# Attention's order from a list of tasks, with tile 2's threshold updates on GpSimd

## The chip, the cores and the metric

The kernel runs on one core of a Trainium2 chip. Its time is the device time of one execution in microseconds, 1262.98 us as the median of three (1262.89 to 1263.99). Five engines work beside each other, each through its own queue in a fixed order, and wait for one another by semaphores: TensorE (PE in the profile, PEld for its weight loads), VectorE (DVE), ScalarE (ACT), GpSimd (POOL) and SyncE (SP, which only issues transfers).

## The reference

One decoder layer on 1024 tokens of width 1024 in float32. A projection of the scaled and shifted input gives queries, keys and values of 8 heads of 64, an indexer's queries and keys, and channels for a causal pool. Attention is sparse: for each query token the indexer scores all earlier tokens, and only the 256 best stay.

```
score = einsum('bqh,bqhs->bqs', w, relu(logits))
score = where(causal, score, -inf)
_, idx = top_k(score, 256)
...
s = einsum('bqhd,bqkhd->bhqk', qb, kg) * HEAD_DIM ** -0.5
p = softmax(where(valid, s, -inf))
o = einsum('bhqk,bqkhd->bqhd', p, vg)
```

Attention and pool are concatenated and multiplied by w_o, then come a layer norm, a SwiGLU feed-forward part and a second layer norm.

## The kernel before

Tokens are cut into eight tiles of 128 (tile i holds tokens 128i to 128i + 127). A tile's 256 best are found as a threshold: 31 bits are settled one after another, each by a count of the scores that reach a candidate, taken over the tile's row of 128(i + 1) scores. `bisect` (line 565) is a Python generator that writes this search step by step; at each `yield` it names the engine of its next piece and a price. `search_v` (596) counts on VectorE and then moves the candidate with two instructions on a column of 128 numbers, `pr` and `cand`; `search_a` (610) does the same on ScalarE. `TILES_A` and `TILES_V` (37) share the tiles out: 3, then 5 and 4 on ScalarE, 7 and 6 on VectorE, and tile 2, alone, on VectorE (`LATE`, 45). Tiles 0 and 1 need no search. When it is done, the scores of the tile hold 0 where a token stays and a large negative number elsewhere, and are added as a mask.

Searches are filled into other work: `Queue` (131) stands in front of every engine, prices each instruction, and before it issues one asks `fill` (697) whether a piece of an open search fits into the engine's idle time. Tile 2's search waits until the one of tiles 7 and 6 is done. What is `pinned` for an engine keeps the order in which it was written; the rest is ordered by the framework's own scheduler, which lets an instruction that is ready pass one that isn't, by its own prices. During attention nothing is pinned.

Attention is 32 units (`units`, 1013): a group g of two tiles (2g + 1 and 2g, from g = 3 down), four head pairs pr in each, and for each pair the two tiles. A unit goes through five steps:

- `u_scores` (1017): TensorE, queries times keys for both heads into a PSUM tile of two banks per head (two such tiles exist, so one unit of tiles 7 to 4 fills both; tiles 3 to 0 take one for both heads).
- `u_exp` (1029): VectorE adds the mask and takes the maximum in one instruction per head, ScalarE the exponential and its sum. `need` (693) first drives the tile's search to its end.
- `u_norm` (1047): VectorE's reciprocal, and GpSimd's multiplication of the probabilities.
- `u_trans` (1055): TensorE transposes blocks of 128, up to four to a PSUM bank, and each bank is copied to `ptb`, every fourth copy by VectorE and the rest by ScalarE.
- `pair_pv` and `pair_cat` (1072, 1082): after both tiles of a pair, TensorE multiplies by the values; ScalarE copies the high part, VectorE makes the low part.

Before these loops only queries of tiles 7 and 6 are ready. `q_make` (934) makes those of the others when group g is under way: the raw rows come back from memory, TensorE transposes them, ScalarE writes four pieces, VectorE two low parts. The places are in `qab` (925); tile 0 shares tile 3's. A matrix product in this kernel takes high and low parts of its operands, so each operand exists twice.

The loop from line 1125 writes the order: scores two units ahead, the finished pair's product, normalisation two units ahead, then this unit's transposes (`STEP_ORDER`, 44). In the last seven units the first blocks of w_o are loaded (`wo_load`, 1092, with GpSimd's multiplication by the gate) and split (`wo_split`, 1097). Behind attention the product with w_o starts (`first`, 1520).

## Time and profile before

| | us |
|---|---|
| median of three runs | 1262.98 |
| profiled execution | 1263.04 |
| its span, first to last instruction | 1261.3 |
| TensorE busy | 1193.2 |
| VectorE busy | 1005.1 |
| ScalarE busy | 662.6 |
| GpSimd busy | 709.0 |

A row of the profile gives the engine, the operation, what it writes and reads (out<-in, with a letter for the area of the on-chip memory), shapes, a count, busy time and mean duration, and the idle time of the engine before it with what ended it. Nearly all rows carry line 174, since every instruction goes through `Queue`; so work is told by its tiles. In attention, `s` are the scores, `sm_H` the probabilities, `pT` and `pT_H` the transposed ones in PSUM and copied, `o` the product with the values, `ws_W` its parts, `qT` and `qab` the queries, `stat_X` maxima and sums. `junk_X`, `keysA_X` and `colsE_X` are tile 2's search, `junkB_X` and `colsA_X` tile 3's. Busy time of TensorE includes the end of each matmul, which the next one overlaps, so a busy TensorE isn't one at its peak.

### The profile page before, as it was taken

Reading aid. Unit: us, or ns where it says so; the run is one execution under the profiler, and the core shown is the slowest. Engines: PE = TensorE matmul, PEld = TensorE weight load, DVE = VectorE, ACT = ScalarE, POOL = GpSimd, SP = SyncE. Lnnn points to the kernel's source line nnn. Section 1 sums busy time; section 2 is a strip of 40 time slices with the busy share of each in tenths; the row PEclk is TensorE's granted clock in tenths of the full one; section 3 lists DMA queues with packets and bytes.
Section 4 is the critical chain, followed back from the end, with each engine's and each line's share of the span. In section 5 each row is a group of like instructions: output and inputs, shape, how many; then the busy total and the mean of one; then the engine's idle time right before and its main releaser. Section 6 shows DMA issues by size and latency. Waiting matters only on the chain.

```text
span 1261.3 us, 16420 instructions
## 1 busy us (share of the span) xinstructions
PE 1193.2 (95%) x5622; PEld 923.9 (73%) x5622; DVE 1005.1 (80%) x1842; ACT 662.6 (53%) x1351; POOL 709.0 (56%) x505
## 2 busy tenths in 40 slices
PE   8999999999888999996889999999999999999996
PEld 6756556687656667885778787878778787878775
DVE  6799997989998765776877868787877778687698
ACT  4667878888785894455443334343333333333521
POOL 0193474675132464285684848384756657486848
PEclk9999999999997999997999999999999999999998
DMA  9610167411000044100202020101111020202112
GB/s 355 240 51 17 58 245 272 155 48 59 17 10 9 26 167 167 60 9 23 102 27 84 32 70 34 67 34 68 39 62 68 34 84 34 84 34 101 63 55 117
DMA packets 32459, 103.40 MB, mean 82 GB/s; under 512 B 3572, under 2 KB 3572, under 8 KB 28792
## 3 DMA queue, kind: packets, MB, share of 16 engines
q1 hardware_dynamic: 32376, 102.36, 22.5%
q8 instruction: 44, 0.72, 0.2%
q14 instruction: 39, 0.32, 0.1%
HBM read 92.90 MB, written 9.45 MB: 81 GB/s over the span
## 4 chain that ended last, share of the span: by engine, by line
PE 63%; DVE 19%; POOL 7%; ACT 6%; issue 5%; DMA 1%; SPq 0%; DVEq 0%; POOLq 0%; ACTq 0%
PE gu L174 23%; PE dn L174 15%; PE pj L174 7%; PE wo L174 4%; DVE junk_X L174 3%; PE pair L174 3%; PE pT L174 2%; DVE act_W L174 2%; PE o L174 2%; PE s L174 2%; DVE utmp_X L174 2%; PE lg L174 2%; POOL wraw_R L174 2%; PE iq L174 1%; DVE stat_C L174 1%
## 5 line engine op out<-in xcount | busy, mean ns | idle before, releaser
L174 PE MATMUL gu<-hr_H,wblk_T 128*128 128x512 f32 (+1 forms) x924 | 217.1, 387 | 5.1 <-ACT gtmp_V L174 4.0
L174 PE MATMUL gu<-hr_H,wblk_V 128*128 128x512 f32 (+1 forms) x924 | 216.3, 386 | 2.4 <-ACT gtmp_V L174 1.8
L174 PEld LDWEIGHTS gu<-hr_H,wblk_T 128*128 128x128 f32 x924 | 171.5, 190 | 41.6 <-ACT gtmp_V L174 4.8
L174 PEld LDWEIGHTS gu<-hr_H,wblk_V 128*128 128x128 f32 x924 | 170.7, 189 | 38.8 <-ACT gtmp_V L174 2.2
L174 DVE TENSOR_TENSOR res_X<-res_X,dn 128x512 f32<-128x512 f32 (+1 forms) x253 | 158.5, 677 | 15.5 <-PE dn L174 15.3
L174 POOL TENSOR_TENSOR wraw_R<-wraw_R 128x512 f32<-128x512 f32 x64 | 94.2, 1480 | 45.8 <-DVE wblk_T L174 23.1
L174 POOL TENSOR_TENSOR wraw_W<-wraw_W 128x512 f32<-128x512 f32 x60 | 86.1, 1442 | 56.8 <-DVE wblk_V L174 28.7
L174 PE MATMUL pj<-ws_W,hT_H 128*128 128x512 f32 x456 | 115.6, 400 | 1.0 <-DVE ws_W L174 1.0
L174 POOL TENSOR_SCALAR sm_H<-sm_H,stat_X 128x1024 f32<-128x1024 f32 (+7 forms) x64 | 48.8, 776 | 113.5 <-PE s L174 42.1
L174 PEld LDWEIGHTS pj<-ws_W,hT_H 128*128 128x128 f32 x456 | 83.0, 188 | 24.9 <-issue 6.6
L174 PE MATMUL dn<-wblk_T,act_W 128*128 128x512 f32 x324 | 79.8, 395 | 2.6 <-DVE act_W L174 1.4
L174 PE MATMUL dn<-wblk_V,act_W 128*128 128x512 f32 x324 | 79.1, 393 | 1.1 <-POOL wblk_V L174 1.1
L174 DVE TENSOR_SCALAR_CACHE_REDUCE junk_X<-keysD_T,colsD_X 128x1024 int16<-128x1024 int16 (+1 forms) x64 | 79.5, 1269 | 0.2
L174 ACT ACTIVATE wblk_V<-wraw_R 128x512 fp32r<-128x512 f32 x56 | 35.2, 629 | 79.5 <-POOL wraw_R L174 66.9
L174 PEld LDWEIGHTS dn<-wblk_T,act_W 128*128 128x128 f32 x324 | 60.6, 189 | 18.3 <-POOL wblk_T L174 3.9
L174 ACT ACTIVATE wblk_V<-wraw_W 128x512 fp32r<-128x512 f32 x53 | 33.1, 628 | 75.1 <-POOL wraw_W L174 61.7
L174 PEld LDWEIGHTS dn<-wblk_V,act_W 128*128 128x128 f32 x324 | 60.1, 188 | 16.6 <-POOL wblk_V L174 3.9
L174 ACT ACTIVATE wblk_T<-wraw_W 128x512 fp32r<-128x512 f32 x56 | 34.9, 627 | 67.2 <-POOL wraw_W L174 56.2
L174 ACT ACTIVATE wblk_T<-wraw_R 128x512 fp32r<-128x512 f32 x52 | 32.5, 627 | 62.0 <-POOL wraw_R L174 52.0
L174 DVE SCALAR_TENSOR_TENSOR score_X<-relu_K,const_C,score_X 128x384 f32<-128x384 f32 (+5 forms) x42 | 54.1, 1289 | 5.0 <-ACT relu_K L174 1.4
L174 ACT ACTIVATE utmp_X<-gu 128x512 f32<-128x512 f32 x33 | 19.8, 599 | 72.7 <-PE gu L174 72.7
L174 ACT ACTIVATE junkA_T<-keys_T,colsA_X 128x768 bf16<-128x768 uint16 (+3 forms) x62 | 54.4, 877 | 3.8 <-DVE colsA_X L174 2.9
(299 smaller groups left out, 2747.0 us busy)
## 6 DMA issues: line engine op xcount, KB each, us to landing
mset_K<-in_wmr_dram SPq DMA_DIRECT2D x16, 1024.0 KB, 5.4
wm_K<-in_wma_dram SPq DMA_DIRECT2D x16, 512.0 KB, 9.9
wraw_R<-in_wg_dram SPq DMA_DIRECT2D x6, 1024.0 KB, 4.8
wraw_R<-in_wd_dram SPq DMA_DIRECT2D x12, 512.0 KB, 3.5
wraw_W<-in_wup_dram SPq DMA_DIRECT2D x12, 512.0 KB, 3.5
wraw_R<-in_wup_dram SPq DMA_DIRECT2D x10, 512.0 KB, 3.6
wraw_W<-in_wg_dram SPq DMA_DIRECT2D x5, 1024.0 KB, 4.9
wraw_W<-in_wd_dram SPq DMA_DIRECT2D x10, 512.0 KB, 3.5
```

The lines of the kernel that those rows point to most:

```text
L174: ins_ = f(*a, **k)
```

## The change

Attention is no longer written by a loop. Every step of every unit, every set of queries and every pair's product becomes a `Task` with an engine, a price, a rank, the tasks that it follows and the PSUM slots that it takes (`Ring`: four of one bank, two of two banks). Searches still open are `Chain`s, whose next step has a rank that spreads what is left of them up to one unit before the tile is wanted. A loop then takes, again and again, what can start first by the prices, and of those that can start at the same time the lowest rank; it writes that one and moves its engine's clock. All of it is pinned on TensorE, VectorE, ScalarE and GpSimd. A copy of transposed blocks goes to either ScalarE or VectorE, VectorE with 0.15 us against it. Queries have a rank 40 below the unit that uses them; tile 0's get a place of their own. The first w_o blocks are written behind attention, not pinned. And the two column instructions that end each step of tile 2's search go to GpSimd.

```diff
 AHEAD = 2
+EAGER = 0
+Q_LEAD = 40
+CHAIN_LEAD = 1
+V_BIAS = 0.15
...
-                    yield "V", 0.3 + 1.08 * w_(i) + (0.35 * nt if m == nt - 1 else 0.0)
+                    yield "V", 0.3 + 1.08 * w_(i) + (0.35 * nt if m == nt - 1 and tiles != LATE else 0.0)
...
                 off = -float(1 << (b - 1)) if b > 0 else -1.0
+                by = V
+                if tiles == LATE:
+                    by = G
+                    yield "G", 0.45
                 for m in range(nt):
-                    V.tensor_scalar(one(pr, m), one(cntc, m), 0.0, float(1 << b), ALU.is_ge, ALU.mult)
+                    by.tensor_scalar(one(pr, m), one(cntc, m), 0.0, float(1 << b), ALU.is_ge, ALU.mult)
                 for m in range(nt):
-                    V.tensor_scalar(one(cand, m), one(pr, m), one(cand, m), off, ALU.add, ALU.add)
+                    by.tensor_scalar(one(cand, m), one(pr, m), one(cand, m), off, ALU.add, ALU.add)
...
-        streams.insert(0, [T.t, next(b), b, a[0], a[0] == LATE])
+        streams.insert(0, [T.t, next(b), b, a[0], a[0] == LATE, a[2], 0])
...
+    class Task:
+
+        def __init__(self, q, cost, rank, emit, deps=(), slots="", late=0.0):
+            self.q, self.cost, self.rank, self.emit, self.deps, self.slots, self.late = q, cost, rank, emit, deps, slots, late
+            self.end, self.kind, self.masks = None, emit.__name__[0:2], ()
+
+    class Ring:
+
+        def __init__(self, n):
+            self.free = [[0.0] for _ in range(n)]
+
+        def ready(self, n):
+            return max((f[0] if f[0] is not None else FAR) for f in self.free[0:n])
+
+        def take(self, n):
+            got = [[None] for _ in range(n)]
+            self.free = self.free[n:] + got
+            return got
...
-    for u in units[0:AHEAD]:
-        u_scores(u)
-        u_exp(u)
+    qab[0] = buf("T", 0, 1536, "qab", F32R)
...
+    def q_rows(t, rank):
...
+        l_ = task("S", 0.1, rank, load, q_turns[-3:-2], late=4.0)
+        t_ = task("T", 0.55, rank, turn, (l_,), "A", late=0.2)
+        c0 = task("A", 1.2, rank, lambda: copies(0), (t_,))
+        lw = task("V", 1.4, rank, lambda: copies(2), (c0,))
+        c1 = task("A", 1.2, rank, lambda: copies(1), (c0,))
+        t_.readers = (c1, lw)
+        t_.masks = {1: (2, 3), 0: (4, 5)}.get(t, ())
...
+        s_t = task("T", 0.1 + 0.0014 * n, 10 * k - EAGER, s_, q_done[i], "B" if n <= 512 else "BB", late=0.2)
+        before = [t for w in where for t in sm_users.get(w, ())]
+        xs = [task("V", 0.08 + 0.00105 * n, 10 * k, lambda e=e: x_(e), [s_t] + before, late=0.12) for e in (0, 1)]
+        for x in xs:
+            x.masks = (i,)
+        s_t.readers = xs
+        es = [task("A", 0.16 + 0.00097 * n, 10 * k + 1, lambda e=e: e_(e), (xs[e],), late=0.15) for e in (0, 1)]
+        r_ = task("V", 0.15, 10 * k + 1, lambda: V.reciprocal(cols["c"][:, 2:4], cols["c"][:, 2:4]), es, late=0.15)
+        ns = [task("G", 0.1 + 0.001 * n, 10 * k + 2, lambda e=e: n_(e), (r_,), late=0.15) for e in (0, 1)]
...
+                p = task("T", 0.107 * m, 10 * k + 3, p_, (ns[e],), "A", late=0.25)
+                c = task("AV", (0.09 + 0.11 * m, 0.09 + 0.13 * m), 10 * k + 3, c_, [p] + list(o_tasks[-2:-1]), late=0.1)
+                p.readers = (c,)
...
+    Q_USE = {5: 8, 4: 9, 3: 16, 2: 17, 1: 24, 0: 25}
+    for t in (5, 4, 3, 2, 1, 0):
+        q_rows(t, 10 * Q_USE[t] - Q_LEAD)
...
+        o_t = task("T", 0.1 + 0.43 * (g + 1), 10 * k + 14, o_, cs, "A", late=0.3)
+        h_t = task("A", 0.3, 10 * k + 15, hi_, (o_t,), late=0.1)
+        l_t = task("V", 0.38, 10 * k + 16, lo_, (h_t,), late=0.1)
...
+    goal = {2: 17, 3: 16, 4: 9, 5: 8, 6: 1, 7: 0}
+    class Chain:
+
+        def __init__(self, st):
+            self.st, self.at, self.n = st, 0.0, -1
+            nt = len(st[3])
+            total = 6 * nt + 1 + (31 * (nt + 1) + 2 if st[5] else 31 * nt)
+            self.left = max(total - st[6], 1)
+            self.goal = max(goal[i] for i in st[3]) - CHAIN_LEAD
+            self.step()
+
+        def step(self):
+            self.n += self.q != "G" if self.n >= 0 else 1
+            self.rank = 10 * self.goal * (self.n + 1) / self.left
+            self.q = self.st[1][0]
+            self.cost = 1.08 * self.st[1][1]
...
-    for st in streams:
-        st[4] = True
-    u_norm(units[0])
-    nxt, nrm = AHEAD, 1
-    for n_, u in enumerate(units):
-        g, pr, i = u
-        for step in STEP_ORDER:
-            if step == "S":
-                while nxt < nu and nxt <= n_ + (AHEAD if units[nxt][0] > 1 else AHEAD_SMALL):
-                    u_scores(units[nxt])
-                    u_exp(units[nxt])
-                    nxt += 1
-            elif step == "P" and i % 2 == 1 and n_ > 0:
-                pair_cat(*units[n_ - 1][0:2], pair_pv(*units[n_ - 1][0:2]))
-            elif step == "N":
-                while nrm < nu and nrm <= n_ + (NORM if units[nrm][0] > 1 else NORM_SMALL):
-                    u_norm(units[nrm])
-                    nrm += 1
-            elif step == "T":
-                u_trans(u)
-        if g > 0 and (pr, i % 2) in Q_AT:
-            t = 2 * (g - 1) + 1 - Q_AT.index((pr, i % 2))
-            q_make(t, q_load(t))
-        if g == 0 and n_ == nu - 7:
-            wo_load(0)
-        if g == 0 and n_ == nu - 5:
-            wo_split(0)
-            wo_load(1)
-            wo_load(2)
-    while streams:
-        advance(streams[0])
+    pinned.update("TVAG")
...
+    def earliest(t, q):
+        at = clock[q]
+        for d in t.deps:
+            if d.end is None:
+                return FAR
+            at = max(at, d.end)
+        for i in t.masks:
+            if i not in masked:
+                return FAR
+            at = max(at, masked[i])
+        if t.slots:
+            at = max(at, rings[t.slots[0]].ready(len(t.slots)))
+        return at
...
+    while todo or chains:
+        best = None
+        for t in todo:
+            if best is not None and t.rank > best[3] + 400:
+                break
+            for n_q, q in enumerate(t.q):
+                at = earliest(t, q)
+                if at >= FAR:
+                    continue
+                key = (at + (V_BIAS if n_q else 0.0), t.rank)
+                if best is None or key < best[0]:
+                    best = key, t, q, t.rank, at, n_q
+        for c in chains:
+            at = max(clock[c.q], c.at)
+            key = (at, c.rank)
+            if best is None or key < best[0]:
+                best = key, c, c.q, c.rank, at, 0
...
+        cost = (t.cost[n_q] if type(t.cost) is tuple else t.cost) + 0.02
+        if q == "T":
+            cost += 0.15 * (kind[0] != t.kind)
+            kind[0] = t.kind
...
+    pinned.clear()
+    wo_load(0)
+    wo_split(0)
+    wo_load(1)
+    wo_load(2)
     times.fill = None
     wo_split(1)
-    pair_cat(0, 3, pair_pv(0, 3))
     wo_split(2)
     for k in range(3, KT):
         wo_load(k)
```

More of the change, by code (lines that the diff above doesn't have):

```diff
@@ L683, in advance @@
             pinned.add(q.name)
+        st[6] += 1
         try:
@@ new lines, in decoder_layer_kernel, with task @@
+    FAR = 1.0e9
+    todo, rings = [], {"A": Ring(4), "B": Ring(2)}
+    def task(*a, **k):
+        todo.append(Task(*a, **k))
+        return todo[-1]
+    nu = len(units)
+    qab[0] = buf("T", 0, 1536, "qab", F32R)
+    sm_of, o = {}, 0
+    for u in units:
+        n = P * (u[2] + 1)
+        if n > 512:
+            sm_of[u] = [smr[:, (o + e) % 6 * 1024 :][:, 0:n] for e in (0, 1)], {o % 6, (o + 1) % 6}
+            o += 2
+        else:
+            sm_of[u] = [smr[:, o % 6 * 1024 + 512 * e :][:, 0:n] for e in (0, 1)], {o % 6}
+            o += 1
@@ new lines, in decoder_layer_kernel, with load, turn, copies @@
+    sm_users, live = {}, {}
+    q_done, q_turns = {7: (), 6: ()}, []
+    masked = {0: 0.0, 1: 0.0}
+    def q_rows(t, rank):
+        hold_ = {}
+        def load():
+            hold_["raw"] = q_load(t)
+        def turn():
+            hold_["pt"] = q_transpose(hold_["raw"])
+        b = qab[t]
+        qa, ql = b[:, 0:1024], b[:, 1024:1536]
+        qops[t] = qa, ql
+        qv = qa.rearrange("p (r e t) -> p r e t", e=2, t=P)
+        lv = ql.rearrange("p (r t) -> p r t", t=P)
+        def copies(lo):
+            pv = hold_["pt"].rearrange("p (r t) -> p r t", t=P)
+            if lo == 0:
+                A.activation(qv[0:64, :, 0, :], pv[0:64], AF.Copy)
+                A.activation(qv[64:128, :, 1, :], pv[64:128], AF.Copy)
+            elif lo == 1:
+                A.activation(qv[64:128, :, 0, :], pv[0:64], AF.Copy)
+                A.activation(qv[0:64, :, 1, :], pv[64:128], AF.Copy)
+            else:
+                V.tensor_tensor(lv[0:64], pv[0:64], f_(qv[0:64, :, 0, :]), ALU.subtract)
+                V.tensor_tensor(lv[64:128], pv[64:128], f_(qv[64:128, :, 1, :]), ALU.subtract)
+        l_ = task("S", 0.1, rank, load, q_turns[-3:-2], late=4.0)
[5 more added lines that the diff above has]
+        t_.masks = {1: (2, 3), 0: (4, 5)}.get(t, ())
+        q_done[t] = (c1, lw)
+        q_turns.append(t_)
@@ new lines, in decoder_layer_kernel @@
+    t0 = T.t
+    clock = {q: max(queues[q].t - t0, 0.0) if q in queues else 0.0 for q in "VAGTS"}
+    hold.clear()
+    times.fill = None
+    pinned.update("TVAG")
+    for i in biased:
+        masked[i] = 0.0
+    chains = [Chain(st) for st in streams]
+    todo.sort(key=lambda t: t.rank)
+    kind = [""]
+    def earliest(t, q):
[11 more added lines that the diff above has]
+        return at
@@ new lines, in run_chain @@
+    def run_chain(c, at):
+        clock[c.q] = at + c.cost
+        c.at = at + c.cost + 0.1
+        before_ = set(biased)
+        advance(c.st)
+        for i in biased - before_:
+            masked[i] = c.at
+        if c.st in streams:
+            c.step()
+        else:
+            chains.remove(c)
+    held_by = {}
+    for t in todo:
+        if t.slots:
+            t.waiting = {id(r) for r in t.readers}
+            for r in t.readers:
+                held_by.setdefault(id(r), []).append(t)
@@ new lines, in decoder_layer_kernel @@
+    while todo or chains:
+        best = None
+        for t in todo:
+            if best is not None and t.rank > best[3] + 400:
[12 more added lines that the diff above has]
+                best = key, c, c.q, c.rank, at, 0
+        _, t, q, _, at, n_q = best
+        if t in chains:
+            run_chain(t, at)
+            continue
+        cost = (t.cost[n_q] if type(t.cost) is tuple else t.cost) + 0.02
+        if q == "T":
+            cost += 0.15 * (kind[0] != t.kind)
+            kind[0] = t.kind
+        if t.slots:
+            t.got = rings[t.slots[0]].take(len(t.slots))
+        t.emit(q) if len(t.q) > 1 else t.emit()
+        clock[q] = at + cost
+        t.end = at + cost + t.late
+        todo.remove(t)
+        for r in list(held_by.get(id(t), ())):
+            r.waiting.discard(id(t))
+            if not r.waiting:
+                for s_ in r.got:
+                    s_[0] = r.last = max(x.end for x in r.readers)
```

52 lines of the change are left out of this document (added).

## The prediction

> **What bounds the kernel now.** I read the page first, then the busy time of each engine over the stretch that the change touches (from the first attention score at 332.0 us to the last matmul of attention before 481.2), then the chain of waits inside it, then single rows of the timeline. The page gives the span, and what the chain that ended last is made of.
>
> ```profile
> span 1261.3 us, 16420 instructions
> PE 63%; DVE 19%; POOL 7%; ACT 6%; issue 5%; DMA 1%; SPq 0%; DVEq 0%; POOLq 0%; ACTq 0%
> ```
>
> The profiled execution took 1263.04 us, so 1.7 us lie around its span; the median of the runs is 1262.98, the same for this purpose. The window view (length, busy time of each engine with its instruction count, granted clock, DMA) cuts attention in three and adds the output projection behind it.
>
> ```profile
> core 0: us, PE busy (x) PEld busy (x) DVE busy (x) ACT busy (x) POOL busy (x), PEclk, DMA share, GB/s
> 332.00:392.00 60.00, 50.70 (x279) 31.74 (x277) 55.15 (x168) 51.89 (x125) 17.33 (x16) 0.94 0.03 10
> 392.00:440.00 48.00, 44.61 (x275) 30.20 (x276) 36.33 (x111) 31.58 (x71) 17.62 (x19) 0.89 0.06 18
> 440.00:481.20 41.20, 39.01 (x279) 26.53 (x279) 26.57 (x99) 35.56 (x107) 25.59 (x35) 1.00 0.43 154
> 481.20:524.00 42.80, 42.80 (x191) 35.44 (x192) 26.43 (x51) 13.21 (x17) 7.54 (x3) 1.00 0.40 136
> ```
>
> Attention is 149.2 us. In the first 60, VectorE is busy 55.15 (92%) and ScalarE 51.89 (86%): softmax masks, the threshold search of tile 2 and that of tile 3 all run there. In the next 48 neither is above 76%, and TensorE runs at a granted clock of 0.89. GpSimd has room throughout. Over the three rows VectorE works 118.05 us and ScalarE 119.03. The chain of waits around 392 shows why the second stretch begins badly (start, length, what).
>
> ```profile
> 391.62 0.17 DVE colsE_X L174
> ...
> 392.06 0.69 DVE junk_X L174 x2
> ...
> 393.89 0.60 DVE qab_W L174
> ...
> 394.54 0.90 PE s L174 x2
> ```
>
> VectorE goes on with steps of tile 2's search (junk_X counts, colsE_X moves the threshold) while the low halves of tile 4's queries, qab_W, stand behind them on the same queue; TensorE wants the queries at once, tile 2 only at 437.38. Its rows, and two narrow windows:
>
> ```profile
> 391.00:394.50 3.50, 0.00 (x0) 0.00 (x0) 3.27 (x11) 1.43 (x4) 0.00 (x0) 0.87 0.00 0
> 394.50:405.00 10.50, 10.46 (x35) 7.31 (x36) 8.19 (x25) 3.89 (x8) 2.91 (x4) 0.55 0.01 2
> 378.00:384.00 6.00, 5.23 (x23) 4.54 (x22) 5.26 (x15) 5.05 (x14) 1.48 (x2) 0.55 0.00 1
> 374.96 0.58 PE L174 MATMUL s<-kr_K,qab_W 128*128 128x512 f32 x2 [0.88 <-ACT colsA_X L174]
> 394.54 0.90 PE L174 MATMUL s<-kr_K,qab_W 64*128 64x512 f32 x2 [3.97 <-DVE qab_W L174]
> 398.90 4.10 PE L174 MATMUL pT<-const_C,sm_H 128*128 128x128 f32 x18
> 430.68 1.31 PE L174 MATMUL pT<-const_C,sm_H 128*128 128x128 f32 x10
> 437.38 0.96 PE L174 MATMUL s<-kr_K,qab_X 128*128 128x384 f32 x3
> ```
>
> TensorE stands for 3.97 us and then gets a clock of 0.55 for 10.5: a transpose takes 4.10/18 = 0.23 us there against 0.13 at 430.68. A milder thinning of its work, with gaps of 0.88 us and less, is followed by 0.55 in 378 to 384.
>
> **The column updates.** Each of the 31 steps of tile 2's search ends with two instructions on a 128x1 column.
>
> ```profile
> 386.28 0.67 DVE L174 TENSOR_SCALAR_CACHE_REDUCE junk_X<-keysA_X,colsE_X 128x384 uint16<-128x384 uint16 x1
> 387.00 0.40 DVE L174 TENSOR_SCALAR colsE_X<-colsE_X 128x1 f32<-128x1 f32 x2
> 387.44 0.67 DVE L174 TENSOR_SCALAR_CACHE_REDUCE junk_X<-keysA_X,colsE_X 128x384 uint16<-128x384 uint16 x1
> L174 DVE TENSOR_SCALAR colsE_X<-colsE_X 128x1 f32<-128x1 f32 (+1 forms) x51 | 9.2, 181 | 1.3
> ```
>
> A step repeats every 387.44 - 386.28 = 1.16 us, of which the count and its read-out keep VectorE about 0.68; moving the update frees 0.48. The last row is the group within 332 to 392: 51 instructions, so some 25 steps and 25 x 0.48 = 12.0 us freed there. That makes ScalarE the fuller one: 55.15 - 12.0 = 43.2 against 51.89. The new list may put a transposed block's copy on either engine (before, every fourth went to VectorE), so the two can meet at (43.2 + 51.9)/2 = 47.5; at the 92% that VectorE now reaches, 47.5/0.92 = 51.7. **Gain 8 us.** Without that sharing, 51.89/0.92 = 56.4, a gain of 3.6. Tile 3's search on ScalarE becomes such a spread chain too; what of it leaves this stretch falls into the next, where ScalarE idles 16 us, and I add nothing for it.
>
> On GpSimd the two instructions have no row of their size. The nearest:
>
> ```profile
> L1875 POOL MEMSET const-float32-0.0<- 128x1 f32 x1 | 0.1, 98 | 0.2 <-issue 0.2
> L174 POOL TENSOR_TENSOR ub_V<-ub_V,const_C 128x16 f32<-128x16 f32 x4 | 1.5, 371 | 0.3
> L174 POOL TENSOR_SCALAR sm_H<-sm_H,stat_X 128x128 f32<-128x128 f32 x8 | 2.9, 370 | 0.5 <-DVE stat_X L174 0.5
> L174 POOL TENSOR_SCALAR sm_H<-sm_H,stat_X 128x1024 f32<-128x1024 f32 x8 | 9.3, 1177 | 51.1 <-PE s L174 39.1 <-DVE colsE_X L174 11.7 <-DVE stat_X L174 0.3
> 385.06 0.16 DVE L174 RECIPROCAL stat_X<-stat_X 128x2 f32<-128x2 f32 x1
> 385.39 2.00 POOL L174 TENSOR_SCALAR sm_H<-sm_H,stat_X 128x896 f32<-128x896 f32 x2 [5.91 <-DVE stat_X L174]
> ```
>
> From below 0.10 (a fill), from above 0.37 each. From 128 to 1024 columns the price grows by 0.807/896 = 0.0009 a column, which leaves 0.25 at one column; I take 0.25, a pair 0.50 (0.20 to 0.74). The hop from VectorE to GpSimd is 385.39 - 385.22 = 0.17, and I take as much back. A step then lasts 0.68 + 0.17 + 0.50 + 0.17 = 1.52 us instead of 1.16, and the search 31 x 1.52 = 47 us and its conversions. The list spreads it until unit 16 of 32, some 80 us into attention, so the longer step is hidden behind masks and copies that VectorE does between two counts. Behind the count that waits stand, in VectorE's fixed order, just those. GpSimd takes 62 x 0.25 = 15.5 us more on 60.5 of 149.2, and each normalisation behind an update waits 0.5: nothing.
>
> **The order.** The list takes whatever can start first, lower rank at equal times. Queries have a rank 40 below the unit that uses them, so tile 4's conversion no longer stands behind the search. The hole is 3.97; the slow clock costs 10.46 x 0.45 = 4.7 in the first window and 5.23 x 0.45 = 2.4 in the other; 11.1 in all. Not all comes back, since what TensorE would reach sooner must come from ScalarE and VectorE: **gain 8 us** (4 to 11). The Trainium skill, page "TensorE: Matmul & The Clock Gate", section "HAM oscillation — how this bites in real kernels", asks only that no idle gap exceed about 3.4 us; by it, a list without such a gap returns the whole 11. The rows here are harsher: the clock fell at 378 with no gap over 0.88 us before it.
>
> Tile 0's queries also move. They shared a buffer with tile 3's and had to wait for its last scores:
>
> ```profile
> 461.23 2.41 ACT L174 ACTIVATE qab_H<-qT 64x512 fp32r<-64x512 f32 x4
> 463.67 1.41 DVE L174 TENSOR_TENSOR qab_H<-qT,qab_H 64x512 fp32r<-64x512 f32 x2 [2.17 <-ACT qab_H L174]
> ```
>
> All 3.8 us are on the chain; with a buffer of their own they are made earlier beside other work: **gain 3** (0 to 4). The query loads move ahead on SyncE's queue with them; that queue has nothing else to carry then.
>
> Against these stand two costs. The list prices a pair's probabilities-times-values at 0.1 + 0.43(g+1) us: 1.82 at g = 3, 0.53 at g = 0. The rows say otherwise:
>
> ```profile
> 385.90 3.45 PE L174 MATMUL o<-pT_H,vf_V 128*64 128x256 f32 x30
> 472.05 0.87 PE L174 MATMUL o<-pT_H,vf_V 128*64 128x256 f32 x8
> ACT ws_W L174 <- PE o L174: 4.6, 5, 1.9
> ```
>
> With 32, 24, 16 and 8 records of 0.11 it is 3.5, 2.6, 1.75 and 0.87. ScalarE's copy of the result stands in its order 1.7, 1.2, 0.8 and 0.3 too early, four times each: 16 us if every wait were laid bare (the last row: 4.6 in sum as it was). Waits fold into one another, and 0.15 us that the list adds at every change of matmul kind runs the other way; I take **2**. The first three output-weight blocks (transfers on SyncE's queue, one GpSimd product each, a copy and a difference) were written among the last units and now follow the list, on queues whose attention instructions are held in order.
>
> ```profile
> L174 POOL TENSOR_TENSOR raw_R<-raw_R,gr_G 128x1024 f32<-128x1024 f32 x5 | 11.9, 2370 | 3.9 <-DMA raw_R<-in_wo_dram 3.0 <-PE pT L174 0.7 <-issue 0.2
> 481.12 42.61 PE wo L174 x187
> ```
>
> They themselves aren't held and can still slip into gaps; their slots come free once the last queries are transposed. If the cover were gone, TensorE would wait 2.4 for a product and about 2.3 for the two halves, 4.7; behind it 42.6 us of matmuls hide the rest. I take **1**.
>
> Sum: 1263.0 - 8 - 8 - 3 + 2 + 1 = **1247**, attention at 133 us. As a check by load: (118.05 - 31 x 0.40 + 119.03)/2 = 112.3 of work on the two engines; 133 would be 84% of them, between the 89% of the first stretch and the 79% of all.
>
> **The rivals.** (1) The list packs better: the 89% of the first stretch everywhere gives 112.3/0.89 = 126, 1240; at 94%, 1233. For it: the stretches from 392 on leave VectorE and ScalarE a quarter idle. Against: they wait for TensorE there. (2) The list only unloads VectorE: occupancy stays at 79%, 112.3/0.79 = 142 us, 1256. The order before was a scheduler's too. (3) The mispriced products are laid bare, 14 more than I took: 1261, no change. For it: ScalarE waited 4.6 us for these products even before. Against: where it has other ready copies queued, the wait is none. (4) Slower: VectorE waits at each count for GpSimd. The plan leaves 0.69 us from a count to the next (0.45 x 1.08 and 0.1 twice). If an update costs 0.37, the answer takes 0.17 + 0.74 + 0.17 = 1.08, 0.39 late in every step, 12 us; and a normalisation just begun (0.37 to 1.18, say 0.8) ahead of half the updates adds 16 x 0.8 = 13. With VectorE as the bound that is 1247 + 25 = 1272. It decides as soon as the answer comes later than the work planned between two counts. For it: 31 round trips on a fixed order. Against: the linear fit, and the masks that can stand between (shortest, median, longest in ns):
>
> ```profile
> L174 DVE CUSTOM_DVE_ANT_0 sm_H<-s,score_X x48: 547/882/1225, 333.8 to 459.5; 128x1024 f32<-128x1024 f32 x8, 128x896 f32<-128x896 f32 x8, 128x768 f32<-128x768 f32 x8, 128x640 f32<-128x640 f32 x8
> ```
>
> The Trainium skill, "GPSIMD Engine Reference", section "3.1 Elementwise — side-by-side cycle accounting", speaks for this one: two software dispatch hops per instruction and elementwise work better left to VectorE; the 128x16 row agrees with a high fixed price.
>
> **How the numbers follow.** Forecast, 1243 to 1252: 0.38; rival 1: 0.24; rival 2: 0.16; rival 3: 0.07; rival 4: 0.15. A change below 0.2% (2.5 us) can't be told from none. Faster: 0.38 + 0.24 + 0.16 = 0.78; same 0.07; slower 0.15. The range runs from rival 1's far end to past rival 3, 1233 to 1263, leaving out rival 4 and a little below.
>
> **What would show it.** Right: attention under 137 us from first score to the unbroken run of wo matmuls; no TensorE idle above 2 us before a score that waits for qab; no window at 0.55 inside; 62 GpSimd rows on colsE_X of about 0.25. Wrong: VectorE idle before junk_X, released by GpSimd, over 5 us in sum (rival 4); ScalarE idle before ws_W for o over 8 us (rival 3; as before would be 4.6); a gap ahead of the first wo matmuls; or a step's gain in the places named that comes back as TensorE idle at g = 1 and 0.

## The result and the profile after

The changed kernel takes 1273.98 us in the median of five runs (1272.71 to 1274.95), 1.0083 times the kernel before, with an interval of 1.0070 to 1.0095. The forecast was 1247; the time lies outside its range, and the kernel is slower. The profiled execution took 1272.71 us. First the page of the changed kernel, its span and the chain that ended last:

```profile
span 1270.9 us, 16425 instructions
...
PE 37%; DVE 7%; POOL 5%; issue 2%; ACT 1%; DVEq 0%; POOLq 0%; ACTq 0%
```

The chain says little here, since its shares add up to about half of the span. The windows say more (length, busy time of each engine with its count, granted clock, DMA), with the same edges as before the change:

```profile
332.00:392.00 60.00, 40.62 (x237) 27.81 (x236) 45.09 (x104) 50.17 (x107) 29.80 (x56) 0.80 0.10 32
392.00:440.00 48.00, 40.23 (x282) 29.43 (x281) 34.03 (x95) 36.23 (x89) 22.09 (x38) 0.89 0.04 12
440.00:481.20 41.20, 38.36 (x248) 25.25 (x249) 24.74 (x92) 32.00 (x87) 20.68 (x26) 0.87 0.28 103
```

And TensorE's rows where attention begins and where the unbroken run of wo matmuls starts:

```profile
333.55 1.73 PE L178 MATMUL s<-kr_K,qab_V 128*128 128x512 f32 x8
...
493.45 3.92 PE L178 MATMUL wo<-wo_V,ws_W 128*128 128x512 f32 x16
```

Attention, from its first score to the unbroken run, goes from 333.55 to 493.45, 159.9 us, where it was 149.1: 10.8 more. It begins 1.6 later, and what follows it is 2.7 shorter; 10.8 + 1.6 - 2.7 = 9.7 is the difference between the two profiled executions (1272.71 - 1263.04). VectorE did lose its column work: 45.09 us busy in the first 60 instead of 55.15. But TensorE is busy only 40.62 of them instead of 50.70, and its granted clock is below that of before in the first and the third window. The waits of the whole stretch (who, whom for; sum, times, longest):

```profile
ACT ws_W L178 <- PE o L178: 14.5, 12, 3.4
...
PEld pT L178 <- POOL colsE_X L178: 11.2, 4, 4.4
...
DVE junk_X L178 <- POOL colsE_X L178: 9.7, 11, 1.8
...
PE pT L178 <- ACT qab_X L178: 6.1, 1, 6.1
```

Two of the signs that the prediction named as wrong are there: VectorE idles 9.7 us before counts, released by GpSimd (over 5), and ScalarE 14.5 before the results of the product (over 8, 4.6 before). VectorE's rows at 351, TensorE's between 349 and 392, and the copies of query sets that these hang on:

```profile
351.36 0.67 DVE L178 TENSOR_SCALAR_CACHE_REDUCE junk_X<-keysA_X,colsE_X 128x384 int16<-128x384 int16 x1 [0.67 <-POOL colsE_X L178]
...
351.96 1.39 DVE L178 TENSOR_TENSOR qab_W<-qT,qab_W 64x512 fp32r<-64x512 f32 x2
354.14 0.67 DVE L178 TENSOR_SCALAR_CACHE_REDUCE junk_X<-keysA_X,colsE_X 128x384 int16<-128x384 int16 x1 [0.80 <-POOL colsE_X L178]
...
355.57 0.67 DVE L178 TENSOR_SCALAR_CACHE_REDUCE junk_X<-keysA_X,colsE_X 128x384 int16<-128x384 int16 x1 [0.75 <-POOL colsE_X L178]
...
357.00 0.67 DVE L178 TENSOR_SCALAR_CACHE_REDUCE junk_X<-keysA_X,colsE_X 128x384 int16<-128x384 int16 x1 [0.75 <-POOL colsE_X L178]
```

```profile
349.46 1.09 PE L178 MATMUL pT<-const_C,sm_H 128*128 128x128 f32 x8
354.72 0.90 PE L178 MATMUL pT<-const_C,sm_H 128*128 128x128 f32 x4 [4.16 <-ACT qab_W L178]
...
360.48 1.08 PE L178 MATMUL pT<-const_C,sm_H 128*128 128x128 f32 x4 [3.62 <-ACT qab_H L178]
...
389.60 0.90 PE L178 MATMUL pT<-const_C,sm_H 128*128 128x128 f32 x3 [6.06 <-ACT qab_X L178]
```

```profile
350.70 1.18 ACT L178 ACTIVATE qab_W<-qT 64x512 fp32r<-64x512 f32 x2
353.38 1.20 ACT L178 ACTIVATE qab_W<-qT 64x512 fp32r<-64x512 f32 x2 [0.85 <-DVE qab_W L178]
...
384.01 1.18 ACT L178 ACTIVATE qab_X<-qT 64x512 fp32r<-64x512 f32 x2
...
386.94 1.38 DVE L178 TENSOR_TENSOR qab_X<-qT,qab_X 64x512 fp32r<-64x512 f32 x2
```

From 355.57 to 357.00 a step of tile 2's search takes 1.43 us (1.16 before), and VectorE stands for 0.75 of them: nothing is written between two counts. A query set goes through three steps: ScalarE's first copy, VectorE's low part, ScalarE's second copy. Until they are made, the set keeps its one-bank PSUM slot, so TensorE's next transposes wait for it, 4.16, 3.62 and 6.06 us. The low part of the first set, at 351.96, stands behind a count that waited, but that isn't what held it: ScalarE's first copy ends only at 351.88. At the third set it does start late, at 386.94, 1.75 us after the first copy (384.01 + 1.18), behind counts that waited and the low part of a w_o block. So these three holes belong in the main to the order; e13, below, has most of them too. The stretches of 3.41 us around the third:

```profile
378.82:382.24 3.42, 3.42 (x26) 2.30 (x23) 2.75 (x9) 2.44 (x5) 3.42 (x3) 1.00 0.00 0
382.24:385.65 3.41, 1.30 (x12) 1.06 (x10) 1.52 (x6) 3.16 (x8) 2.42 (x6) 1.00 0.01 2
385.65:389.06 3.41, 0.00 (x0) 0.00 (x0) 3.08 (x4) 1.07 (x4) 2.85 (x4) 0.50 0.26 70
389.06:392.48 3.42, 1.71 (x7) 1.34 (x8) 2.64 (x7) 3.33 (x9) 2.01 (x5) 0.50 0.21 84
392.48:395.89 3.41, 3.41 (x16) 3.30 (x15) 2.27 (x7) 2.15 (x6) 2.18 (x4) 0.50 0.00 0
395.89:399.30 3.41, 3.41 (x32) 2.15 (x32) 2.50 (x7) 2.92 (x6) 0.72 (x2) 1.00 0.02 5
```

TensorE is busy 1.30 of 3.41 us, and the next three such stretches have a clock of 0.50, the last of them with TensorE at work throughout, 16 records where the full clock has 32. In the clock records every period at half clock is a whole multiple of 3.41 us, apart from the last of a trace, which outlasts the kernel. In attention they add up to 47.8 us, against 17.1 before the change.

### The profile page after: what moved, and what is told of

It reads as the page before. It is cut to its first block, busy times and chain, and to the rows that moved or that the text cites. A ratio compares the mean times of both kernels' runs of the same rounds, so it can differ in the third digit from the quotient of the medians.

```text
span 1270.9 us, 16425 instructions
## 1 busy us (share of the span) xinstructions
PE 1190.3 (94%) x5622; PEld 925.5 (73%) x5622; DVE 991.3 (78%) x1771; ACT 669.1 (53%) x1360; POOL 726.6 (57%) x567
## 4 chain that ended last, share of the span: by engine, by line
PE 37%; DVE 7%; POOL 5%; issue 2%; ACT 1%; DVEq 0%; POOLq 0%; ACTq 0%
PE gu L178 23%; PE dn L178 15%; DVE act_W L178 2%; DVE utmp_X L178 2%; POOL wraw_R L178 1%; POOL wblk_T L178 1%; POOL wraw_W L178 1%; POOL wblk_V L178 1%; DVE gtmp_V L178 1%; DVE wblk_T L178 1%; DVE hr_H L178 0%; POOL hr_H L178 0%; DVE stat_C L178 0%; DVE wblk_V L178 0%; DVE res_X L178 0%
## 5 line engine op out<-in xcount | busy, mean ns | idle before, releaser
L178 POOL TENSOR_TENSOR wraw_W<-wraw_W 128x512 f32<-128x512 f32 x60 | 85.8, 1437 | 55.1 <-DVE wblk_V L178 27.3
L178 PE MATMUL pT<-const_C,sm_H 128*128 128x128 f32 x288 | 48.4, 314 | 24.1 <-ACT qab_X L178 6.1
L178 PEld LDWEIGHTS pT<-const_C,sm_H 128*128 128x128 f32 x288 | 36.2, 158 | 36.9 <-POOL colsE_X L178 11.2
## 6 DMA issues: line engine op xcount, KB each, us to landing
wm_K<-in_wma_dram SPq DMA_DIRECT2D x16, 512.0 KB, 10.2
```

The lines of the kernel that those rows point to most:

```text
L178: ins_ = f(*a, **k)
```

## The experiments

Two theories stood at the start. R: the round trip of each search step over GpSimd costs the time. A: the list itself does, with query sets taken too early or products priced too low. A third, C, came out of the windows above: much of it is the clock. In the expectations of e1 to e4, B is R, and what is called A here is split: A for the query sets, C for the product's price; from e9 on, C is the clock, as in the text. O is the order, whoever makes the update. The ratio compares with the kernel before on the same chip; there it took 1262.98 to 1264.90 us, so that medians of different rows can be off by some 2 us against each other. The two right columns come from each kernel's profiled execution.

| run | median us | ratio (interval) | attention us | of it at half clock |
|---|---|---|---|---|
| before | 1262.98 | 1 | 149.1 | 17.1 |
| after | 1273.98 | 1.0083 (1.0070 to 1.0095) | 159.9 | 47.8 |
| e1 late queries | 1273.26 | 1.0062 (1.0040 to 1.0084) | 159.5 | 58.0 |
| e2 updates on VectorE | 1259.67 | 0.9962 (0.9950 to 0.9974) | 144.5 | 23.9 |
| e3 product's price | 1265.93 | 1.0011 (0.9999 to 1.0023) | 153.1 | 34.1 |
| e4 update alone | 1274.76 | 1.0086 (1.0062 to 1.0111) | 160.1 | 41.0 |
| e5 GpSimd beside | 1260.08 | 0.9956 (0.9942 to 0.9971) | 144.7 | 23.9 |
| e6 room after step | 1262.82 | 0.9991 (0.9976 to 1.0006) | 147.9 | 27.3 |
| e7 VectorE and price | 1267.79 | 1.0025 (1.0014 to 1.0036) | 154.4 | 44.4 |
| e8 VectorE, price, late | 1259.21 | 0.9958 (0.9944 to 0.9973) | 150.5 | 41.0 |
| e9 filled gaps | 1266.07 | 1.0017 (1.0004 to 1.0029) | 153.0 | 10.2 |
| e10 VectorE, filled | 1264.46 | 1.0004 (0.9994 to 1.0015) | 149.3 | 6.8 |
| e11 VectorE, room | 1267.14 | 1.0026 (1.0010 to 1.0042) | 152.3 | 37.5 |
| e12 update twice | 1277.39 | 1.0102 (1.0085 to 1.0119) | 166.5 | 51.2 |
| e13 changed order, VectorE | 1267.44 | 1.0027 (1.0014 to 1.0041) | 159.3 | 47.8 |
| e14 VectorE's order, GpSimd | 1267.24 | 1.0029 (1.0015 to 1.0044) | 152.9 | 41.0 |
| e15 late and price, GpSimd | 1257.98 | 0.9959 (0.9945 to 0.9973) | 145.8 | 23.9 |
| e16 VectorE, partly filled | 1268.20 | 1.0031 (1.0016 to 1.0046) | 153.7 | 30.7 |

Four profiled executions are the longest of their kernels, e8 (1264.08), e13 (1272.44), e15 (1260.76) and e16 (1269.89), and three the shortest, after (1272.71), e4 (1273.54) and e10 (1261.58); their right columns needn't fit the medians.

### Undoing one part, or doing it alone

**Late queries** (e1): a set is transposed only after the scores three units ahead of its use.

```diff
...
+    for t, t_ in turn_of.items():
+        t_.deps += (s_of[Q_USE[t] - 3],)
```

> The changed kernel, but the transposes of a query set may not go before the scores of the unit three ahead of the one that uses them. Theory A (query sets transposed as soon as they can hold up to three of the four one-bank PSUM slots, and the transposes of probabilities wait behind them): TensorE's four long waits that end with a qab copy (4.2, 3.6, 6.1 and 2.2 us, 16 in all) go, the time falls from 1274 to 1258 to 1264. Theory B (VectorE's waits for GpSimd's column updates, 9.7 us): stays within 1270 to 1276. Theory C (the product with the values priced at half, ScalarE's waits for it 14.5 us against 4.6 before): within 1270 to 1276.

1273.26: nothing clear gained (2.7 us by the ratios, whose intervals overlap). TensorE now waits 16.9 us before scores for maxima still to be taken of earlier ones (stat_X), where the changed kernel has 5.5.

**Updates on VectorE** (e2): the list stays, the two column instructions return.

```diff
-                    yield "V", 0.3 + 1.08 * w_(i) + (0.35 * nt if m == nt - 1 and tiles != LATE else 0.0)
+                    yield "V", 0.3 + 1.08 * w_(i) + (0.35 * nt if m == nt - 1 else 0.0)
...
-                if tiles == LATE:
-                    by = G
-                    yield "G", 0.45
```

> The changed kernel with the column updates of tile 2's search back on VectorE. Theory A: the queries still hold the slots, 1270 to 1278. Theory B: the 9.7 us of waits go, 12 us of update work come back beside idle time, 1262 to 1266. Theory C: 1272 to 1276.

1259.67, faster than both, and below what any of the three theories gave. Its first two windows:

```profile
332.00:392.00 60.00, 41.93 (x218) 27.30 (x217) 51.83 (x149) 50.92 (x110) 17.32 (x14) 0.80 0.10 32
392.00:440.00 48.00, 45.46 (x344) 31.69 (x343) 40.36 (x121) 40.13 (x98) 21.28 (x21) 1.00 0.04 12
```

The first is as thin for TensorE as in the changed kernel; from 392 on the clock is whole, and 344 matmul records fall into the second where the changed kernel has 282.

**The product's price** (e3):

```diff
-        o_t = task("T", 0.1 + 0.43 * (g + 1), 10 * k + 14, o_, cs, "A", late=0.3)
+        o_t = task("T", 0.1 + 0.86 * (g + 1), 10 * k + 14, o_, cs, "A", late=0.3)
```

> The changed kernel with the list's price of the product with the values doubled, 0.1 + 0.86(g + 1). Theory A: the waits for qab stay, 1270 to 1276. Theory B: 1270 to 1276. Theory C: ScalarE's waits for the product fall from 14.5 to about 5 us and the time to 1262 to 1266.

1265.93, 8 us less. ScalarE's wait for the product falls from 14.5 to 3.2 us over the same stretch.

**The update alone** (e4): the kernel before, with only the column updates on GpSimd. The prices at the search's yields change with them, so what is filled in between can differ too.

> The kernel before with only the column updates moved to GpSimd. If VectorE has other work in each round trip, as the prediction had it, the first stretch gains up to 8 us: 1255 to 1260. Theory B, the round trip laid bare: a step of 1.43 us against 1.16 in places where nothing else is ready, 31 x 0.27 = 8 us longer, 1263 to 1271.

1274.76, as slow as the whole change and more than either theory gave. The waits of this kernel:

```profile
DVE junk_X L174 <- POOL colsE_X L174: 16.0, 19, 2.3
...
PE s L174 <- DVE qab_W L174: 7.2, 1, 7.2
```

Nineteen counts wait for GpSimd, and the hole before the queries of tile 4, 3.97 us before the change, is 7.2: VectorE comes to qab_W later. This is the first evidence for R in an order that the list did not write.

### What of the update costs

**GpSimd beside** (e5): e2 with the same two instructions also on GpSimd, on columns that nobody reads.

```diff
+                if tiles == LATE:
+                    G.tensor_scalar(spare[:, 1:2], spare[:, 0:1], 0.0, float(1 << b), ALU.is_ge, ALU.mult)
+                    G.tensor_scalar(spare[:, 2:3], spare[:, 1:2], spare[:, 2:3], off, ALU.add, ALU.add)
```

> The list with the column updates back on VectorE (that kernel took 1259.7), and in each of the 31 steps GpSimd also makes the same two 128x1 instructions on columns of its own, for which nobody waits; the list does not price them, so the written order is the same. The outputs are the reference's. Theory R (what costs 14 us is the round trip: VectorE's next count has to wait for an answer from another engine): nothing hangs on GpSimd here, 1259 to 1262. Theory G (62 more instructions on GpSimd delay the normalisations, or GpSimd's small instructions slow VectorE's): most of the 14 comes back, 1268 to 1274, and TensorE's wait for sm_H grows.

1260.08 against 1259.67: the 62 instructions cost nothing where nobody waits for them. Neither the time that they take on GpSimd nor their neighbourhood to VectorE is the matter.

**Room after a step** (e6): the list waits 0.5 us instead of 0.1 after GpSimd's update.

```diff
-        c.at = at + c.cost + 0.1
+        c.at = at + c.cost + (0.5 if c.q == "G" else 0.1)
```

> The changed kernel with one constant of the list: after GpSimd's update the next count of a search may be taken 0.5 us later instead of 0.1, so that the list leaves 1.09 us of VectorE's time between two counts where it left 0.69, and the answer, measured at 0.75, is there in time. Theory R in the form of my fourth rival (the answer comes later than the work planned between two counts): the wait of junk_X for colsE_X falls from 9.7 to under 3 us and the time to 1262 to 1268. Theory P (the wait itself is harmless, but the search now ends 8 us later or more, and everything of tile 2 and behind it comes late): slower still, 1274 to 1282, because the search ends at about 437 instead of 425.

1262.82, 11 us less, and the wait of the counts falls from 9.7 to 2.5 us, as R says. The same room with updates on VectorE is the control (e11):

```diff
+        c.at = at + c.cost + (0.5 if c.st[3] == LATE else 0.1)
```

> The list with the column updates on VectorE and the same 0.5 us of room between two steps of tile 2's search that brought 11 us with the updates on GpSimd. Theory R (room helped because GpSimd's answer then came in time): no gain here, 1258 to 1263. If it helped because the search was spread thinner, leaving VectorE to others: 1250 to 1256. If any change of a constant moves the time by several us through the clock, it may come out at 1265 as well.

1267.14, 7.5 us more than e2. So room helped only where an answer had to come from GpSimd, but the control shows too that one constant moves this schedule by 7 us; why it does, no run shows.

**The update twice** (e12): two more instructions between pr and cand.

```diff
+                if tiles == LATE:
+                    G.tensor_scalar(one(pr, 0), one(pr, 0), 1.0, 0.0, ALU.mult, ALU.add)
+                    G.tensor_scalar(one(pr, 0), one(pr, 0), 1.0, 0.0, ALU.mult, ALU.add)
```

> The changed kernel with two more 128x1 instructions on GpSimd in each of the 31 steps, between pr and cand (they multiply pr by one), unpriced by the list, so in the same order. The outputs are the reference's. The answer comes 2 x 0.3 = 0.6 us later. Theory R (VectorE waits out the answer in most steps): the wait of junk_X for colsE_X grows from 9.7 us toward 28, and the time by 10 to 19 us, 1284 to 1293. If the round trip is mostly covered: under 5 us, 1274 to 1279.

The group of counts' waits, and two counts of one stretch:

```profile
DVE junk_X L178 <- POOL colsE_X L178: 20.0, 14, 2.5
```

```profile
355.42 0.67 DVE L178 TENSOR_SCALAR_CACHE_REDUCE junk_X<-keysA_X,colsE_X 128x384 int16<-128x384 int16 x1 [1.30 <-POOL colsE_X L178]
...
357.39 0.67 DVE L178 TENSOR_SCALAR_CACHE_REDUCE junk_X<-keysA_X,colsE_X 128x384 int16<-128x384 int16 x1 [1.30 <-POOL colsE_X L178]
```

A bare step now takes 1.97 us, 0.54 more, and the waits add up to 20.0, 10.3 more; the time rises by 3.4, to 1277.39. R in the form that sums waits is wrong: some two thirds of the longer waits are absorbed.

### Order or engine

**Price with VectorE** (e7) joins e2 and e3:

> The list, column updates on VectorE (1259.7 by itself), and the product with the values priced at 0.86 a tile pair instead of 0.43 (with updates on GpSimd that brought 8 us). If the two costs add: 1250 to 1254. If the price only helped because it made room in which GpSimd's answers came: no gain here, 1258 to 1262.

1267.79, above both forecasts: the price that gained 8 us with updates on GpSimd loses 8 here. With the query sets held back as well (e8):

> As the run with updates on VectorE and the doubled price, and no query set is transposed before the scores three units ahead of its use, so that no query set keeps a one-bank slot of PSUM while it waits for ScalarE and VectorE. If early query sets cost slots: 3 to 5 us under that run. If not, as with updates on GpSimd (1273.3 against 1274.0): within 2 us of it.

1259.21; and the same two constants with the updates on GpSimd (e15):

> The list with the product priced at 0.86 a tile pair and the query sets held back to three units ahead of their use, with the column updates on GpSimd as in the changed kernel. With the updates on VectorE these two constants gave 1259.2. Theory R: 1268 to 1274. Theory O (every constant throws the order anew, within some 8 us either way): anything from 1256 to 1274, and no fixed distance from 1259.2.

1257.98. At these constants, where each engine's update comes with an order of its own, no difference can be told, and the changed kernel with two constants altered is faster than the one before. So neither "the price was wrong" nor "the queries came too early" is a cause with a size of its own: alone they gave -8 and 0, together -16, and on VectorE's side +8 and then 0. That left open whether the 14 us between the changed kernel and e2 are the round trip or the order. The two missing corners: e13 writes the changed kernel's order but lets VectorE make the updates in it, e14 writes e2's order but lets GpSimd make them.

```diff
 e13
-                    by = G
 e14, against the version with updates on VectorE
-                by = V
+                by = G if tiles == LATE else V
```

> The changed kernel with the order that its list wrote (updates planned as if on GpSimd), but VectorE itself makes the two column instructions, at the place in its order where the list would have sent them to GpSimd; the rest of each engine's order is the same. Theory R (the round trip costs the 14 us: the wait for GpSimd is gone, 0.48 us of VectorE takes its place in each step): 1259 to 1264. Theory O (the order that the list writes once a search step is planned as two pieces with a pause is the bad one, whoever makes the update): 1270 to 1276.

> The other corner: the order that the list writes with updates on VectorE (1259.7), but GpSimd makes them, unplanned; VectorE and the rest stand in the same order. Theory R: the answer comes 0.27 us later than VectorE's own in every step, and where nothing stands between two counts all of 0.75 us is idle: 1266 to 1274. Theory O: 1258 to 1263, since VectorE has 0.48 us less to do in each step.

| | made by GpSimd | made by VectorE |
|---|---|---|
| order with the step planned in two pieces | 1273.98 | 1267.44 |
| order with the step planned on VectorE | 1267.24 | 1259.67 |

Both theories hold half, and e13 lies between their ranges. The engine is worth 6.5 and 7.6 us, the order 6.7 and 7.8 (by the ratios 7.1 and 8.5, 6.8 and 8.2). Since one constant moves this schedule by 7 to 8 us (e7, e11), the order's part is no price of planning a step in two pieces; why that order is the worse one stays open.

What the engine does is seen in e14, whose order is that of e2. One query set, first in e2, then in e14:

```profile
384.43 1.39 DVE L178 TENSOR_TENSOR qab_T<-qT,qab_T 64x512 fp32r<-64x512 f32 x2
385.86 1.19 ACT L178 ACTIVATE qab_T<-qT 64x512 fp32r<-64x512 f32 x2 [0.69 <-DVE qab_T L178]
387.10 4.83 PE L178 MATMUL o<-pT_H,vf_V 128*64 128x256 f32 x32 [1.93 <-ACT qab_T L178]
```

```profile
383.96 0.67 DVE L178 TENSOR_SCALAR_CACHE_REDUCE junk_X<-keysA_X,colsE_X 128x384 uint16<-128x384 uint16 x1 [1.83 <-POOL colsE_X L178]
385.65 0.67 DVE L178 TENSOR_SCALAR_CACHE_REDUCE junk_X<-keysA_X,colsE_X 128x384 uint16<-128x384 uint16 x1 [1.00 <-POOL colsE_X L178]
388.45 0.67 DVE L178 TENSOR_SCALAR_CACHE_REDUCE junk_X<-keysA_X,colsE_X 128x384 uint16<-128x384 uint16 x1 [2.12 <-POOL colsE_X L178]
389.16 1.39 DVE L178 TENSOR_TENSOR qab_T<-qT,qab_T 64x512 fp32r<-64x512 f32 x2
390.59 1.19 ACT L178 ACTIVATE qab_T<-qT 64x512 fp32r<-64x512 f32 x2 [4.36 <-DVE qab_T L178]
391.83 6.05 PE L178 MATMUL o<-pT_H,vf_V 128*64 128x256 f32 x32 [5.14 <-ACT qab_T L178]
```

Behind three counts that wait for GpSimd, the low part comes at 389.16 instead of 384.43, ScalarE's second copy waits for it, and TensorE's product starts 4.73 us later than in e2 (the transposes before it 1.1). The product then takes 6.05 us instead of 4.83, since half clock lasts until 397.1 (389.9 in e2). One more such wait, 4.16 us, holds a mask, and scores that e2 starts at 406.13 start at 414.63. Over the whole of attention e14 is 8.4 us longer, 152.9 against 144.5. That longest wait, and the group:

```profile
410.02 2.38 POOL L178 TENSOR_TENSOR raw_R<-raw_R,gr_G 128x1024 f32<-128x1024 f32 x1
412.49 0.62 POOL L178 TENSOR_SCALAR colsE_X<-colsE_X 128x1 f32<-128x1 f32 x2
413.15 0.67 DVE L178 TENSOR_SCALAR_CACHE_REDUCE junk_X<-keysA_X,colsE_X 128x384 uint16<-128x384 uint16 x1 [4.16 <-POOL colsE_X L178]
DVE junk_X L178 <- POOL colsE_X L178: 17.2, 15, 4.2
```

The bare round trip is 0.75 us. The longer waits are those in which the update stands on GpSimd behind a normalisation or the product for a block of w_o: five of the fifteen, 10.1 of the 17.2 us.

The trace of e13 can't do the same for the changed order, since it is that kernel's longest execution, as long as the changed kernel's (1272.44 and 1272.71), with the same 47.8 us at half clock. TensorE's holes at the three query sets are shorter in it, 2.67 + 3.44 + 4.77 = 10.9 us instead of 13.8, but the transposes behind them start later than in the changed kernel, by 0.24 to 0.55 us:

```profile
355.14 1.09 PE L178 MATMUL pT<-const_C,sm_H 128*128 128x128 f32 x4 [2.67 <-ACT qab_W L178]
...
360.72 1.09 PE L178 MATMUL pT<-const_C,sm_H 128*128 128x128 f32 x4 [3.44 <-ACT qab_H L178]
...
390.15 0.90 PE L178 MATMUL pT<-const_C,sm_H 128*128 128x128 f32 x3 [4.77 <-ACT qab_X L178]
```

So where the 6.5 us lie isn't shown. Ten executions of e13, one and the same program, ran from 1263.59 us at a mean granted clock of 0.980 to 1272.44 at 0.969. Its two at 0.969 took 1272.07 and 1272.44, the changed kernel's two at that clock 1272.71 and 1273.98; but at 0.974 e13 took 1267.13 to 1267.79, and the changed kernel at 0.973 took 1272.92. At one clock of 0.975, e14 took 1267.12 to 1269.97 and e2 1258.86 to 1261.26. The clock moves the executions of one program, but in e2's order the cost of the round trip stands at equal clock too.

### The clock

**Filled gaps** (e9): the changed kernel, its other engines' order untouched; 169 transposes of the identity at eleven places (tasks 2 and 8 of the table had no free place; the expectation counts 163 at ten) go where TensorE's trace had holes, into parts of PSUM tiles that nobody reads.

```diff
+    FILL = {2: 11, 8: 5, 11: 29, 13: 25, 14: 5, 35: 42, 36: 8, 65: 7, 69: 15, 70: 7, 78: 14, 83: 7, 124: 10}
...
+    def fillers(n):
+        ok = [ap for ring, at_, ap in spots if len(ps_ring[ring]) - at_ < {"ps1": 4, "ps2": 2}[ring]]
+        for _ in range(n if ok else 0):
+            T.transpose(ok[-1], ident, ident)
```

> The changed kernel, every instruction of VectorE, ScalarE and GpSimd in the same order; TensorE alone gets 163 more transposes of the identity, written into parts of PSUM tiles that nobody reads, at the ten places where its trace shows TensorE idle for 0.6 us or more (29 of them ahead of the transposes that waited 4.16 us for qab_W, and so on, about 0.85 of each gap). The outputs are the reference's. Theory C (much of the 11 us is not the idle time but the clock: in the trace TensorE's clock falls to one half for whole multiples of 3.41 us after a stretch of 3.41 us in which it was busy less than about 0.6; attention spends 48 us so instead of 17): the half-clock time falls below 25 us, attention from 160 to under 152, the time to 1262 to 1268, though TensorE has 20 us more to do. Theory W (TensorE idles because the others are late, and what runs at half clock would only wait the sooner): no gain, 1272 to 1280.

Its windows, and the first large filling:

```profile
332.00:392.00 60.00, 51.31 (x357) 39.44 (x356) 45.44 (x105) 51.12 (x109) 30.89 (x56) 0.94 0.09 32
392.00:440.00 48.00, 41.19 (x324) 31.72 (x323) 35.24 (x100) 36.35 (x90) 22.60 (x40) 0.96 0.03 12
440.00:481.20 41.20, 40.06 (x298) 27.46 (x298) 24.86 (x100) 34.31 (x101) 22.67 (x34) 1.00 0.36 129
```

```profile
351.51 4.73 PE L178 MATMUL s<-const_C 128*128 128x128 f32 x29
356.08 0.93 PE L178 MATMUL pT<-const_C,sm_H 128*128 128x128 f32 x7
```

The clock is up from 0.80, 0.89 and 0.87 to 0.94, 0.96 and 1.00, the half-clock time in attention falls from 47.8 to 10.2 us, and the kernel is 8 us faster for useless work, though that work itself delays the transposes behind it (356.08 instead of 354.72). This shows, as far as one order can, that the clock too makes up part of the loss. As a way to a faster kernel it fails. In e2's order (e10):

> The same with the list that has its column updates on VectorE (1259.7): 116 transposes of the identity at most, where that kernel's trace shows TensorE idle. Its attention had 24 us at half clock, worth 12 us at most. Theory C: 1252 to 1257, under both kernels. Theory W: 1259 to 1264.

1264.46, 5 us slower than without, though only 6.8 us were left at half clock (in its shortest execution): its 110 transposes cost more than they gave. With 67 (e16):

> The list with the column updates on VectorE (1259.7) and 67 transposes of the identity, only in the seven places where its trace shows TensorE idle for over 1 us, leaving 0.8 us of each idle; the run with 116 came to 1264.5, its attention at half clock for 7 us instead of 24. Theory C with the fillers' own time on the path: the half clock stays under 12 us and the time comes to 1255 to 1259. If a filler costs as much as it saves: 1260 to 1264.

1268.20, and 30.7 us at half clock in its longest execution, more than e2's 23.9: other stretches fall. Theory C's forecast was wrong for both.

Over the thirteen profiled executions of kernels with the list and without fillers, attention goes with the half-clock time as 132.5 us + 0.54 of it (correlation 0.91). That fit is a description, not a proof: waits that thin TensorE's work lengthen attention and lower the clock at once. The kernel before lies 7.4 us above it (132.5 + 0.54 x 17.1 = 141.7, measured 149.1). Read as a cause, it would say that the list packs better at equal clock and loses that to 30.7 us more at half clock (0.54 x 30.7 = 16.6; 16.6 - 7.4 = 9.2 of the 10.8 us); with e10 and e16 against it, that isn't shown.

## Why the prediction was wrong

- **The column updates: gain 8.** This step failed. The durations were near (305 ns in the median where 0.25 us was taken, 1.43 us a step where 1.52 was), and VectorE was relieved by 10.1 us in the first window where 12.0 were forecast:

```profile
L178 POOL TENSOR_SCALAR colsE_X<-colsE_X x62: 220/305/522, 336.3 to 425.6; 128x1 f32<-128x1 f32 x62
```

  What failed is the sentence that the longer step is hidden behind masks and copies that VectorE does between two counts. By its own numbers the answer was late (0.17 + 0.50 + 0.17 = 0.84 us where the plan left 0.69), and the sum has no term for that. Measured, the bare answer takes 0.75, and the rows at 355 show counts with nothing between them. Behind a waiting count stand not only masks and copies but, in the fixed order, the low part of a query set: in e14 that makes a product 4.73 us late; in the changed kernel itself 1.75 us are seen, at the third set (0.79 in e13, where nothing waits for GpSimd). With the order held, the engine of the update costs 6.5 to 7.6 us where a gain of 8 stood.
- **The fourth rival**, with the chance of 0.15, named this mechanism and came to 1272; its price did not hold. It summed 12 + 13 us of late answers; the waits are 9.7 in all, doubling them costs a third of what they grow by, and half of the 14 us between the changed kernel and e2 is the order. Its second term, an update that finds GpSimd at other work, is seen, in e14 above all. That its time was near is luck, since about as much was lost in a place that it did not name.
- **The order: gain 8, and 3 for tile 0.** Failed as well. With updates on VectorE, the changed order still takes 1.0027 times the kernel before, 3 us more where 11 less stood; in the list's own order for it (e2) it is 5 less. The holes did not go; they moved from the scores to the transposes, which wait for slots that query sets hold. What tile 0's own buffer gave was not measured by itself.
- **The clock.** The prediction weighed a rule of an idle gap of 3.4 us against a harsher row. The rule is that of the Trainium skill, "TensorE: Matmul & The Clock Gate", section "HAM oscillation — how this bites in real kernels", no idle gap over about 3.4 us; here the clock fell at 385.65, when TensorE had stood for 2.11 us (of 6.06 in the end). The row was right, but the sum used only that the list would close holes, not that it could open others. The term that was left out is half-clock time, 30.7 us more of it in the profiled executions; what that cost in time isn't shown apart from the waits.
- **The product's price: loss 2.** ScalarE's wait came, 14.5 us instead of 4.6, as the third rival said. A price twice as high brought 8 us in one order and cost 8 in another, so no size can be put to this term.
- **The w_o blocks: loss 1.** What follows attention was 2.7 us shorter, not longer; the blocks' own part was not measured.
- **The check by load** (112.3 us of work in 133) held no term for a wait between two engines inside one dependent chain, and none for the clock.

## What to carry to other kernels

Moving a short instruction of a serial chain to an idle engine trades its duration for a round trip and for the work that stands before it there: count what stands in the fixed order between the two halves of a step, at the places where the order is thinnest, before the relief is booked as a gain. For a list scheduler of work like this, count also the stretches in which TensorE falls under some 60% of 3.4 us and not its idle time alone: over thirteen schedules attention was longer by about 1.8 us with each stretch at half clock (0.54 x 3.41, a correlation). And where changing a constant moves the time by 7 us either way, compare an edit at several settings, or hold the order fixed as e13 and e14 do, before giving it a size.

## What the runs showed of the hardware

In all eighteen traces TensorE's clock changes at marks 3.413 us apart that don't start with the kernel. The stretches between these marks, from 326 to 700 us, were counted by TensorE's busy share. At full clock, 72 of 72 under 0.40 busy were followed by half clock, 52 of 96 between 0.40 and 0.60, and 2 of 1555 from 0.60 on. At half clock, 109 of 109 under 0.80 were followed by another, 19 of 36 between 0.80 and 0.99, and 12 of 121 above. So one long gap isn't needed: in the kernel before, a stretch that had no gap over 0.88 us (373.13 to 376.54, 0.59 busy) went down, and no stretch came back with TensorE busy for less than 0.80 of it. The Trainium skill, "TensorE: Matmul & The Clock Gate", "Part 1: The HAM clock gate (the "warmup" mystery)", has a free-running window of 3413 ns and two clock states; the traces agree with both (3.413 us; records of 0.5 and 1.0 alone). Transposes of the identity kept the clock up (e9: 47.8 us at half clock fell to 10.2). GpSimd's 128x1 instruction took 220 to 522 ns, and from a count's end to the next count by way of two of them VectorE stood 0.75 us where GpSimd was idle.
